# A decoder layer's MLP: the two product chains of a pair of column tiles get PSUM tiles of their own, the first down weights go into the scheduler's order, and a second down tile is begun at each seam

## The chip, the cores and the metric

The kernel runs on one NeuronCore of a Trainium2 chip. The metric is the device time of one execution in microseconds (us), the median of several runs. TensorE (PE) multiplies matrices, VectorE (DVE) and ScalarE (ACT) work element by element, GpSimd (POOL) and SyncE (SP) issue transfers. Each engine works off its own list of instructions, and waits on semaphores for the others.

## The reference, cut to what matters

One layer of a hybrid decoder trunk is applied to 512 prompt tokens and 32 sample tokens. Two mixers and their merge come first, then an MLP with a squared ReLU. The change touches the MLP alone:

```
D_MODEL = 1024
SEQ = 512
DEC_BATCH = 8
DEC_SEQ = 4
D_FF = 4 * D_MODEL
...
    x = x + rms_norm(merged @ w_out, norm_mix_post)
    h2 = rms_norm(x, norm_mlp_pre)
    m = jnp.square(jax.nn.relu(h2 @ w_up)) @ w_down
    x = x + rms_norm(m, norm_mlp_post)
```

Everything is float32.

## The kernel before, in words

Activations lie transposed: 128 channels on the partitions, the 544 tokens along the free axis, in two halves of 272 (`HT`). A float32 product is made of three matmuls on a high and a low part of each operand (`wh`, `wl` of a weight, `bh`, `bl` or `a0h`, `a0l` of an activation): high by high, high by low, low by high. So each weight tile, once it has landed as `wt_...`, is prepared in two steps: ACT copies it into the high part (`cut`, line 1264, "CAST wh"), and DVE subtracts to get the low part (`rest`, line 71, "wl").

`w_up` has 32 column tiles of 128. The first eight are made in the plain way (tiles `ps_u` at lines 116 and 126), scheduled by the framework's list scheduler. From there on the code stands under `tc.manual_schedule`, which keeps each engine's instructions in the order in which the code is written. The rest of `w_up` is done for pairs of column tiles (index `q`, 4 to 15) with seven products instead of eight: `P1` to `P7`, 12 matmuls each (line 1311). They form three accumulation chains. Chain X (P1, P6, P7, P4) and chain Y (P5, P3) lie in one PSUM tile of two banks, `XY[q]`, X in bank 0 and Y in bank 1; chain Z (P2) has a bank of its own. Between the products ACT and DVE read what has accumulated (`keep`, `c11`, `c12`, `c22`, `row1_b`). The order on TensorE for one pair is P6, P1 of the next pair, P7, P2 of the next, P4, P3, P5 of the next. `row1_b` is the ACT instruction at line 1361 that reads X once P4 has ended.

PSUM has two pools: `psd` with two tiles of two banks (`dense_tile`) and `pss` with four tiles of one bank (`scratch`). A dense tile is taken in turn by X/Y of a pair and by the down tiles.

After every four pairs, 1024 rows of the hidden layer are there, and a down pass multiplies them with `w_down`: eight output tiles `m`, each one PSUM tile `ps_d`, eight steps `k` of six matmuls (`d_part`, line 116). `d_load`, `d_cut` and `d_rest` load and prepare the weights of a tile, `d_out` adds the result to what earlier passes gave (ACT copies it in pass 0). There are passes 0 to 3; pass 0 follows the plain part, and pass 3 is of half depth, four steps `k` per tile, and shares a prepared weight between two tiles. The place where the last pair (`p = q + 3`) hands over to the next down pass is called a seam here; there are three. At a seam, steps `k` = 0 to 5 of down tile 0 are interleaved with the last pair's products; steps 6 and 7 need what the last pair yields: `c12` on DVE, `row0`, `act_hi` on ACT, `act_lo` on DVE (the last writes `a0l`).

At the head of the manual part, pass 0 begins. Before its first tile the code writes the loads and the preparation of tile 0, and four DVE instructions on whole quarters (128x1088 elements: `tt_`, `f12`, `f21`), which are operands of the seven products.

Of the kernel before, what the change touches and what calls it, by code (L numbers as in the profile page):

```python
# [13 lines left out]
AF = mybir.ActivationFunctionType  # L14
# [6 lines left out]
NT = 544  # L21
HT = 272
# [23 lines left out]
def layer(ctx, tc, a, o):  # L46
# [1202 lines left out]
    with tc.tile_pool(name="up", bufs=1, reuse_waits="tile") as up:  # L1249
# [50 lines left out]
        def lo(n, q):  # L1300
            W[n, q] = rest(*W[n, q], f"{n}{q}", "b" if n == "B" else "w")

        XY, Z, CP, R = {}, {}, {}, {}

        def product(ps, n, q, half, b, first, last):
            h, l = (w[:, 512 * half:512 * half + 512] for w in W[n, q])
# [4 lines left out]
                    mm(ps, lhsT=w[:, c], rhs=x_[:, k], start=(first and k == 0 and j == 0), stop=(k == 3 and j == 2), skip_group_check=True)  # L1311

        def P1(q):
            XY[q] = dense_tile(f"ps_u{q}")
            product(XY[q][:, 0, 0:HT], "A", q, 0, hb[0, 0], True, False)

        def P2(q):
            Z[q] = scratch(f"ps_uz{q}")[:, 0:HT]
            product(Z[q], "A", q, 1, hb[0, 1], True, True)

        def P3(q):
            product(XY[q][:, 1, 0:HT], "S34", q, 1, hb[1, 1], False, True)

        def P4(q):
            product(XY[q][:, 0, 0:HT], "B", q, 0, tb[4], False, True)

        def P5(q):
            product(XY[q][:, 1, 0:HT], "S12", q, 0, tb[1], True, False)

        def P6(q):  # L1330
            product(XY[q][:, 0, 0:HT], "S12", q, 1, tb[2], False, False)

        def P7(q):
            product(XY[q][:, 0, 0:HT], "S34", q, 0, tb[3], False, False)

        def keep(n, q):
            c = CP[n, q] = up.tile([P, HT], F32, tag=n, name=f"{n}_{q}", bufs=2 if n == "c1" else 1)
            S.copy(c, XY[q][:, 0, 0:HT])

        def res(q):  # L1340
            R[q] = up.tile([P, 2, NT], F32, tag="t", name=f"t_{q}", bufs=2)
# [2 lines left out]
            tt(R[q][:, 0, 0:HT], CP["c1", q], Z[q], ADD)  # L1344

        def c12(q):
            tt(R[q][:, 0, HT:NT], CP["u2", q], XY[q][:, 1, 0:HT], ADD)

        def c22(q):
            tt(R[q][:, 1, HT:NT], CP["u3", q], XY[q][:, 1, 0:HT], ADD)  # L1350

        ak = lambda q, i: ah_[(2 * q + i) % 8]

# [4 lines left out]
            S.activation(R[q][:, 1, HT:NT], R[q][:, 1, HT:NT], AF.Relu, scale=-1.0)  # L1358

        def row1_b(q):  # L1360
            S.activation(R[q][:, 1, 0:HT], XY[q][:, 0, 0:HT], AF.Relu, scale=-1.0)  # L1361
            S.activation(R[q][:, 1], R[q][:, 1], AF.Square)

        def act_hi(q, i):
# [28 lines left out]
        def d_out(c, m):  # L1393
# [3 lines left out]
            else:  # L1397
                tt(mv, ps[:, :, 0:HT], mv, ADD)

        with tc.manual_schedule(engines={ET.PE, ET.Activation, ET.DVE, ET.SP, ET.Pool}):  # L1400
            d_load(0, 0)
            d_load(0, 1)
            d_cut(0, 0)
            d_rest(0, 0)
            d_load(0, 2)

            f11, f21, f12, f22 = (ov[:, 4 * kh:4 * kh + 4, HF[hf]] for hf in range(2) for kh in range(2))
            tt_ = [up.tile([P, 4, HT], F32, tag="t", name=f"tt{i}", bufs=2) for i in range(2)]
            tt(tt_[0], f11, f12, SUB)
            stt(tt_[1], tt_[0], -1.0, f22, MUL, SUB)  # L1410
            tt(f12, f22, f12, SUB)
            stt(f21, tt_[1], -1.0, f21, MUL, SUB)
            d_part(0, 0, *range(8))
            d_cut(0, 1)
            d_rest(0, 1)
            split(*tb[3], f12)
            split(*tb[4], f21)
            d_part(0, 1, *range(8))
            d_load(0, 3)
            d_cut(0, 2)  # L1420
            d_rest(0, 2)
            split(*tb[1], tt_[0])
            d_out(0, 0)
            split(*tb[2], tt_[1])
            d_out(0, 1)
            for c in range(3):

                ms = range(2 if c == 0 else 0, 8)
                q = 4 * c + 4
                nxt = {3: [lambda: load_a(q), lambda: load_s12(q), lambda: load_s34(q), lambda: load_b(q)],  # L1430
                       5: [lambda: add_s(q), lambda: hi("A", q), lambda: lo("A", q), lambda: load_a(q + 1)],
                       6: [lambda: hi("S12", q), lambda: lo("S12", q), lambda: load_s12(q + 1)],
                       7: [lambda: hi("B", q), lambda: lo("B", q), lambda: load_s34(q + 1), lambda: load_b(q + 1)]}
                for m in ms:
                    if m + 2 < 8 and not (c == 0 and m + 2 < 4):
                        d_load(c, m + 2)
                    if m + 1 < 8:
                        if not (c == 0 and m + 1 < 3):
                            d_cut(c, m + 1)
                            d_rest(c, m + 1)  # L1440
                    if c == 0 or m > 1:
                        d_part(c, m, *range(8))
                    elif m == 0:
                        d_part(c, 0, 6, 7)
                    else:
                        d_part(c, 1, *range(8))
                    for f in nxt.get(m, ()):
                        f()
                    d_out(c, m)

                P1(q)
                keep("c1", q)
                P2(q)
                res(q)
                hi("S34", q)
                lo("S34", q)
                hi("A", q + 1)
                c11(q)
                lo("A", q + 1)
                P5(q)  # L1460
                load_a(q + 2)
                for p in range(q, q + 4):
                    n, nn, e = p + 1 < q + 4, p + 2 < q + 4, p == q + 3
                    P6(p)
                    if p > q:
                        hi("B", p)
                        act_hi(p - 1, 0)
                        lo("S34", p)
                    keep("u2", p)
                    if p > q:  # L1470
                        lo("B", p)
                        act_lo(p - 1, 0)
                    if nn:
                        load_s12(p + 2)
                    if n:
                        P1(p + 1)
                        keep("c1", p + 1)
                        add_s(p + 1)
                    if nn:
                        load_s34(p + 2)  # L1480
                        load_b(p + 2)
                    if not n:
                        d_part(c + 1, 0, 0, 1)
                    P7(p)
                    keep("u3", p)
                    c22(p)
                    if n:
                        hi("S12", p + 1)
                        P2(p + 1)
                        res(p + 1)  # L1490
                        c11(p + 1)
                        lo("S12", p + 1)
                    else:
                        d_part(c + 1, 0, 2, 3)
                    row1_a(p)
                    if nn:
                        hi("A", p + 2)
                    P4(p)
                    row1_b(p)
                    if nn:  # L1500
                        lo("A", p + 2)
                    P3(p)
                    act_hi(p, 1)
                    c12(p)
                    row0(p)
                    if p + 3 < q + 4:
                        load_a(p + 3)
                    if n:
                        hi("S34", p + 1)
                        P5(p + 1)  # L1510
                    act_lo(p, 1)
                    if p == q + 1:
                        d_load(c + 1, 0)
                    if p == q + 2:
                        d_load(c + 1, 1)
                        d_cut(c + 1, 0)
                        d_rest(c + 1, 0)
                act_hi(q + 3, 0)
                act_lo(q + 3, 0)
                if c < 2:  # L1520
                    d_part(c + 1, 0, 4, 5)

            wd = []
            xr = {}
            w47 = big.tile([P, 4, 2, 512], F32R, tag="yhg", name="wd47")
            for m in range(8):
                t = mp.tile([P, 2, 512], F32R, tag=f"bl{m // 2}{m % 2}", name=f"wd{m}") if m < 4 else w47[:, m - 4]
                wd.append((t[:, 0], t[:, 1]))
            wt = {}
            for m in range(8):  # L1530
                j = m // 2
                if m % 2 == 0:
                    if j < 2:
                        d_load(3, j + 2)
                    if j < 3:
                        d_cut(3, j + 1)
                        d_rest(3, j + 1)
                    wt[j] = raw(a["w_down2"][1, j].rearrange("p a b c -> p (a b c)"), f"e{j}")
                if m:
                    d_part(3, m, *range(4))  # L1540
                if m % 2:
                    for i in range(2):
                        split(*wd[m - 1 + i], wt[j][:, 512 * i:512 * i + 512])
                d_out(3, m)
                if m > 3:
                    hf, kh = divmod(m - 4, 2)
                    xr[hf, kh] = mp.tile([P, 4, HT], F32, tag=f"bh{hf}{kh}", name=f"xr{hf}{kh}")
                    nc.sync.dma_start(out=xr[hf, kh], in_=x1_d[:, 4 * kh:4 * kh + 4, HF[hf]])
# [152 lines left out]
```

## Time and profile before

| | before |
|---|---|
| median of 3 runs | 988.1 us (988.02 to 989.58) |
| the profiled execution | 985.89 us |
| its span, first to last instruction | 983.9 us |
| PE busy | 952.3 us, 97% |
| DVE busy | 621.6 us, 63% |
| ACT busy | 446.9 us, 45% |
| mean granted TensorE clock | 0.994 |
| share of PE in the chain that ended last | 90% |

The span is what the profile shows instruction by instruction; some 2 us of the execution lie outside it. Matmuls are pipelined, so that PE is shown as busy for longer than the pitch at which matmuls start: a matmul of 272 columns is listed with 290 ns, and the next starts 125 ns after it.

### The profile page before, as it was taken

The page shows a single profiled execution, that of the slowest core. Times are in us where ns is not written, and L with a number is a line of the kernel's source. Part 1 is how long each engine was busy: PE and PEld are TensorE (multiplying, and loading weights), DVE is VectorE, ACT ScalarE, POOL GpSimd, SP SyncE. Part 2 cuts the span into 40 slices and gives each one's busy share as a digit, 9 for nine tenths or more (in the row PEclk, how much of TensorE's full clock was granted, in tenths as well). Part 3 has the DMA queues.
Part 4 walks back from the last instruction along what each step waited for, and adds up shares of the span by engine and source line. Part 5 has one row for each costly group of instructions (what it writes and reads, how often), then busy time and mean ns, then how long its engine had stood idle before and what let it go on. Part 6 is the DMA issues. An engine that isn't in the chain of part 4 may idle for free.

```text
span 983.9 us, 21362 instructions
## 1 busy us (share of the span) xinstructions
PE 952.3 (97%) x9120; PEld 926.6 (94%) x9120; DVE 621.6 (63%) x1158; ACT 446.9 (45%) x834; POOL 62.6 (6%) x104
## 2 busy tenths in 40 slices
PE   8999999999999999999999999899999999999995
PEld 5999999999999999999999999899989998999894
DVE  6877669496774867666477476543753475447647
ACT  6644363644535333663244475333651165126523
POOL 2100000000000001520100000001100110010000
PEclk9999999999999999999999999999999999999998
DMA  7342142242423438554522512444534463355502
GB/s 257 97 132 69 64 156 66 71 131 71 130 66 106 152 130 293 165 183 178 157 70 87 189 43 92 150 103 113 150 115 110 121 153 114 97 138 142 176 2 91
DMA packets 45406, 121.26 MB, mean 123 GB/s; under 512 B 9120, under 2 KB 12576, under 8 KB 44672
## 3 DMA queue, kind: packets, MB, share of 16 engines
q1 hardware_dynamic: 37664, 97.20, 30.8%
q0 software_dynamic: 7360, 22.15, 8.7%
q8 instruction: 71, 1.16, 0.5%
q10 hardware_dynamic: 288, 0.56, 0.2%
q14 instruction: 23, 0.19, 0.1%
HBM read 101.66 MB, written 17.06 MB: 121 GB/s over the span
## 4 chain that ended last, share of the span: by engine, by line
PE 90%; DVE 4%; ACT 3%; issue 1%; DMA 1%; SPq 0%; DVEq 0%; ACTq 0%
PE ps_in L116 27%; PE ps_d L116 17%; PE ps_u L1311 11%; PE ps_u L126 7%; PE ps_bh L116 5%; PE ps_o L116 2%; PE ps_e L126 2%; PE ps_o L126 2%; PE ps_bs L116 2%; PE psL L643 2%; PE ps_uz L1311 2%; PE ps_u L116 1%; PE psO L709 1%; PE psK L693 1%; PE psT L558 1%
## 5 line engine op out<-in xcount | busy, mean ns | idle before, releaser
L116 PE MATMUL ps_in<-hh,wh_in 128*128 128x272 f32 x736 | 159.2, 297 | 0.0
L116 PE MATMUL ps_in<-hl,wh_in 128*128 128x272 f32 x736 | 153.0, 289 | 0.0
L116 PE MATMUL ps_in<-hh,wl_in 128*128 128x272 f32 x736 | 152.3, 288 | 0.0
L116 PEld LDWEIGHTS ps_in<-hh,wh_in 128*128 128x128 f32 x736 | 115.3, 189 | 2.9 <-issue 1.6
L116 PEld LDWEIGHTS ps_in<-hh,wl_in 128*128 128x128 f32 x736 | 115.7, 188 | 0.0
L116 PEld LDWEIGHTS ps_in<-hl,wh_in 128*128 128x128 f32 x736 | 115.6, 189 | 0.0
L71 DVE TENSOR_TENSOR wl_in<-wt_in,wh_in 128x1024 fp32r<-128x1024 f32 (+1 forms) x54 | 61.7, 1144 | 60.6 <-ACT wh_in L99 57.8
L116 PE MATMUL ps_d<-a0h,wh_d 128*128 128x272 f32 x448 | 93.9, 291 | 5.9 <-ACT wh_d L1264 4.2
L116 PE MATMUL ps_d<-a0l,wh_d 128*128 128x272 f32 x448 | 94.2, 292 | 0.5 <-DVE a0l L71 0.5
L116 PE MATMUL ps_d<-a0h,wl_d 128*128 128x272 f32 x448 | 93.7, 291 | 0.5 <-DVE wl_d L71 0.5
L99 ACT CAST wh_in<-wt_in 128x1024 fp32r<-128x1024 f32 x46 | 48.3, 1052 | 97.8 <-PE ps_in L116 93.3
L116 PEld LDWEIGHTS ps_d<-a0h,wh_d 128*128 128x128 f32 x448 | 71.1, 190 | 7.0 <-ACT wh_d L1264 4.7
L116 PEld LDWEIGHTS ps_d<-a0l,wh_d 128*128 128x128 f32 x448 | 71.0, 190 | 0.9 <-DVE a0l L71 0.9
L116 PEld LDWEIGHTS ps_d<-a0h,wl_d 128*128 128x128 f32 x448 | 71.0, 190 | 0.7 <-DVE wl_d L71 0.7
L71 DVE TENSOR_TENSOR ov<-ps_d,ov 128x544 f32<-128x544 f32 x24 | 17.4, 724 | 60.6 <-PE ps_d L116 60.6
L71 DVE TENSOR_TENSOR wl_d<-wt_d,wh_d 128x1024 fp32r<-128x1024 f32 x28 | 34.1, 1219 | 20.8 <-ACT wh_d L1264 20.8
L1264 ACT CAST wh_d<-wt_d 128x1024 fp32r<-128x1024 f32 x28 | 28.7, 1048 | 29.1 <-PE ps_d L116 23.8
L71 DVE TENSOR_TENSOR t<-u,ps_u 128x272 f32<-128x272 f32 x24 | 10.5, 438 | 43.1 <-PE ps_u L1311 27.1
L71 DVE TENSOR_TENSOR wl_S<-wt_S,wh_S 128x1024 fp32r<-128x1024 f32 x24 | 29.3, 1220 | 11.4 <-ACT wh_S L1264 11.4
L1311 PE MATMUL ps_u<-bh,wh_S 128*128 128x272 f32 x96 | 29.0, 302 | 5.8 <-ACT t L1361 5.8
L676 DVE COPY_PREDICATED scT<-masks,psL 32x128 f32<-32x128 uint8 x80 | 28.3, 354 | 2.3 <-PE psS L646 0.2
L1264 ACT CAST wh_S<-wt_S 128x1024 fp32r<-128x1024 f32 x24 | 25.2, 1048 | 10.1 <-PE ps_d L116 10.1
(540 smaller groups left out, 2340.6 us busy)
## 6 DMA issues: line engine op xcount, KB each, us to landing
wt_in<-in_w_in SPq DMA_DIRECT2D x52, 512.0 KB, 3.6
wt_d<-in_w_down SPq DMA_DIRECT2D x28, 512.0 KB, 3.8
wt_A<-in_w_up SPq DMA_DIRECT2D x12, 512.0 KB, 4.0
wt_S<-in_w_up SPq DMA_DIRECT2D x24, 256.0 KB, 2.8
wt_S<-in_w_up POOLq DMA_DIRECT2D x24, 256.0 KB, 4.4
s<-in_hg_s SPq DMA_DIRECT2D x8, 512.0 KB, 3.8
out_hg_s<-s SPq DMA_DIRECT2D x8, 512.0 KB, 4.2
wt_bh<-in_w_br_hg SPq DMA_DIRECT2D x8, 512.0 KB, 3.7
```

Of the source, the lines that this page charges most:

```text
L71: (e or V).tensor_tensor(out=out, in0=x, in1=y, op=op)
L99: S.copy(wh, wt)
L116: mm(ps[:, i, 0:int(np.prod(x[i].shape[1:]))], lhsT=w[:, c], rhs=x[i], start=st, stop=sp)
L126: mm(ps[:, i, 0:HT], lhsT=ws[i][j][:, c], rhs=x[hf], start=st, stop=sp)
L558: nc.tensor.transpose(pt[:, w], src[:, i, w * P:(w + 1) * P], ident)
L643: mm(pq[sq * y:sq * y + m, 4 * i + w], lhsT=k[:, i, c:c + m], rhs=up(c, c + sq, i), start=True, stop=True)
L676: V.copy_predicated(blocks(sc[r], h)[:, :, y, :, 1], masks[r, L].rearrange("p x (n h) -> p x n h", h=h), pq[r].rearrange("p x (n h) -> p x ...
L693: mm(pk[:, w], lhsT=kt2[:, i, w], rhs=vt[:, i, w], start=True, stop=True)
L709: mm(po[:, w], lhsT=sc[:, i, c], rhs=vt[:, i, w], start=True, stop=(w == 0))
L1264: S.copy(h, t)
L1311: mm(ps, lhsT=w[:, c], rhs=x_[:, k], start=(first and k == 0 and j == 0), stop=(k == 3 and j == 2), skip_group_check=True)
```

## The change

X keeps a dense tile, of which it now uses only the first bank; Y moves into a one-bank tile of the other pool, `ps_uy`, taken in P5. The preparation of down tiles 0 and 1 of pass 0 leaves the manual part and goes ahead of it under `high_priority`, so that the list scheduler places it. At each seam the preparation of down tile 1 moves to a place between `row1_a` and P4 of the last pair. In passes 1 and 2, steps 0 to 5 of down tile 1 are put ahead of steps 6 and 7 of down tile 0.

```diff
-            XY[q] = dense_tile(f"ps_u{q}")
-            product(XY[q][:, 0, 0:HT], "A", q, 0, hb[0, 0], True, False)
+            X[q] = dense_tile(f"ps_u{q}")[:, 0, 0:HT]
+            product(X[q], "A", q, 0, hb[0, 0], True, False)
...
-            product(XY[q][:, 1, 0:HT], "S34", q, 1, hb[1, 1], False, True)
+            product(Y[q], "S34", q, 1, hb[1, 1], False, True)
...
-            product(XY[q][:, 1, 0:HT], "S12", q, 0, tb[1], True, False)
+            Y[q] = scratch(f"ps_uy{q}")[:, 0:HT]
+            product(Y[q], "S12", q, 0, tb[1], True, False)
...
+        with tc.high_priority(offset=WAHEAD):
+            for m in range(2):
+                d_load(0, m)
+                d_cut(0, m)
+                d_rest(0, m)
+            d_load(0, 2)
         with tc.manual_schedule(engines={ET.PE, ET.Activation, ET.DVE, ET.SP, ET.Pool}):
-            d_load(0, 0)
-            d_load(0, 1)
-            d_cut(0, 0)
-            d_rest(0, 0)
-            d_load(0, 2)
...
             d_part(0, 0, *range(8))
-            d_cut(0, 1)
-            d_rest(0, 1)
...
                     elif m == 0:
+                        d_part(c, 1, *range(6))
                         d_part(c, 0, 6, 7)
                     else:
-                        d_part(c, 1, *range(8))
+                        d_part(c, 1, 6, 7)
...
                     row1_a(p)
                     if nn:
                         hi("A", p + 2)
+                    if not n:
+                        d_cut(c + 1, 1)
+                        d_rest(c + 1, 1)
                     P4(p)
```

What the scheduler makes of the head of pass 0 stands in no line of the diff. On DVE, at the end of the plain part, the list before has the low part of the first down weight (`wl_d_0`) directly behind the last activation `a0l`:

```order
L71 TENSOR_TENSOR a0l_7266<-t_u_8050,a0h_7265 128x544
L71 TENSOR_TENSOR wl_d_0_8074<-wt_d_0_8068,wh_d_0_8072 128x1024
L71 TENSOR_TENSOR tt_8078<-ov 128x1088
L74 SCALAR_TENSOR_TENSOR tt_8079<-tt_8078,ov 128x1088
L71 TENSOR_TENSOR ov<-ov 128x4x272
L74 SCALAR_TENSOR_TENSOR ov<-tt_8079,ov 128x4x272
L71 TENSOR_TENSOR wl_d_1_8135<-wt_d_1_8070,wh_d_1_8133 128x1024
```

At the same place of DVE's list the changed kernel has:

```order
L71 TENSOR_TENSOR a0l_7266<-t_u_8050,a0h_7265 128x544
L71 TENSOR_TENSOR tt_8082<-ov 128x1088
L74 SCALAR_TENSOR_TENSOR tt_8083<-tt_8082,ov 128x1088
L71 TENSOR_TENSOR ov<-ov 128x4x272
L74 SCALAR_TENSOR_TENSOR ov<-tt_8083,ov 128x4x272
L71 TENSOR_TENSOR wl_d_0_8070<-wt_d_0_8066,wh_d_0_8068 128x1024
L71 TENSOR_TENSOR bl_6966<-ov,bh_6965 128x1088
L71 TENSOR_TENSOR wl_d_1_8076<-wt_d_1_8072,wh_d_1_8074 128x1024
```

`wl_d_0` has moved behind the four instructions on quarters. On ACT the cast `wh_d_0` keeps its place behind the last `a0h`; on PE and SP nothing moves here.

On PE, where P4 of pair 4 ends and its P3 begins (`wh_B` is P4's weight, `bh` and `bl` with `wh_S` are P3's operands), the list before reads, with the semaphores that an instruction waits for behind it:

```order
L1311 MATMUL ps_u_8564<-t_8065,wh_B_8554 128x272 x2
L1311 MATMUL ps_u_8564<-t_8065,wl_B_8556 128x272
L1311 MATMUL ps_u_8564<-bh_6967,wh_S_8593 128x272 [waits Activation_49]
L1311 MATMUL ps_u_8564<-bl_6968,wh_S_8593 128x272
L1311 MATMUL ps_u_8564<-bh_6967,wl_S_8595 128x272
```

And in the changed kernel:

```order
L1311 MATMUL ps_u_8564<-t_8065,wh_B_8554 128x272 x2
L1311 MATMUL ps_u_8564<-t_8065,wl_B_8556 128x272
L1311 MATMUL ps_uy_8602<-bh_6967,wh_S_8593 128x272 [waits DVE_49]
L1311 MATMUL ps_uy_8602<-bl_6968,wh_S_8593 128x272
L1311 MATMUL ps_uy_8602<-bh_6967,wl_S_8595 128x272
```

The products stand in the same order; P3 writes another tile, and waits for DVE (`c22`, the last reader of Y) instead of ACT.

On ACT at the first seam (`u_7` are the `keep` copies of the last pair, `t` the `row1` instructions, `a0h` the high parts of its results), before:

```order
L1338 COPY u_7_9043<-ps_u_8894 128x272
L1358 ACTIVATE t_8941<-t_8941 128x272
L1361 ACTIVATE t_8941<-ps_u_8894 128x272
L1362 ACTIVATE t_8941<-t_8941 128x544
L1365 CAST a0h_7265<-t_8941 128x544
L1365 CAST a0h_7263<-t_8941 128x544
L1264 CAST wh_d_1_9105<-wt_d_1_8990 128x1024
```

And in the changed kernel:

```order
L1339 COPY u_7_9047<-ps_u_8897 128x272
L1359 ACTIVATE t_8944<-t_8944 128x272
L1264 CAST wh_d_1_9063<-wt_d_1_8994 128x1024
L1362 ACTIVATE t_8944<-ps_u_8897 128x272
L1363 ACTIVATE t_8944<-t_8944 128x544
L1366 CAST a0h_7265<-t_8944 128x544
L1366 CAST a0h_7263<-t_8944 128x544
```

The cast of the second down weight has moved ahead of the read of X; its low part moves on DVE in the same way, from behind the last `a0l` to between `c22` and `c12`. On PE, 18 pairs of matmuls of `ps_d_1` (steps 0 to 5) now stand ahead of the six pairs of `ps_d_0` that need the last pair's results. In pass 3, PE's list keeps its order.

## Rows read from the trace of the kernel before

**Rows 1.** Waits of PE, 600 us to the end: total us, times, longest.

```profile
PE ps_u L1311 <- ACT t L1361: 5.8, 12, 0.5
```

**Rows 2.** Timeline of PE, head of pass 0: start us, us, instruction, idle before.

```profile
629.13 0.41 PE L116 MATMUL ps_u<-bh,wl_u 128*128 128x272 f32 x2
632.69 0.52 PE L116 MATMUL ps_d<-a0h,wh_d 128*128 128x272 f32 x2 [3.15 <-ACT wh_d L1264]
...
633.95 0.82 PE L116 MATMUL ps_d<-a0h,wl_d 128*128 128x272 f32 x2 [0.49 <-DVE wl_d L71]
...
635.02 0.65 PE L116 MATMUL ps_d<-a0l,wh_d 128*128 128x272 f32 x2
635.48 0.66 PE L116 MATMUL ps_d<-a0h,wl_d 128*128 128x272 f32 x2
```

**Rows 3.** Windows there: length, PE, PEld, DVE, ACT, POOL busy, clock, DMA share, GB/s.

```profile
634.00:636.00 2.00, 2.00 (x9) 2.00 (x10) 1.97 (x2) 0.00 (x0) 0.00 (x0) 0.50 0.54 106
636.00:638.00 2.00, 2.00 (x14) 2.00 (x14) 2.00 (x3) 0.34 (x1) 0.00 (x0) 0.72 0.42 164
```

**Rows 4.** Timeline of ACT, head of pass 0.

```profile
631.60 1.99 ACT L1264 CAST wh_d<-wt_d 128x1024 fp32r<-128x1024 f32 x2
```

**Rows 5.** Timeline of DVE, head of pass 0.

```profile
632.67 1.23 DVE L71 TENSOR_TENSOR wl_d<-wt_d,wh_d 128x1024 fp32r<-128x1024 f32 x1 [0.22 <-ACT wh_d L1264]
633.82 1.28 DVE L71 TENSOR_TENSOR tt<-ov 128x1088 f32<-128x1088 f32 x1
...
638.75 1.22 DVE L71 TENSOR_TENSOR wl_d<-wt_d,wh_d 128x1024 fp32r<-128x1024 f32 x1
```

**Rows 6.** Timeline of PE, end of P4 and start of P3, pair 4.

```profile
695.54 0.29 PE L1311 MATMUL ps_u<-t,wl_B 128*128 128x272 f32 x1
696.31 0.39 PE L1311 MATMUL ps_u<-bh,wh_S 128*128 128x272 f32 x1 [0.49 <-ACT t L1361]
696.54 0.29 PE L1311 MATMUL ps_u<-bl,wh_S 128*128 128x272 f32 x1
```

**Rows 7.** Timeline of ACT there: `row1_b` reading X.

```profile
695.86 0.40 ACT L1361 ACTIVATE t<-ps_u 128x272 f32<-128x272 f32 x1 [0.43 <-PE ps_u L1311]
```

**Rows 8.** Timeline of DVE there: `c22`, the last reader of Y.

```profile
693.25 0.44 DVE L71 TENSOR_TENSOR t<-u,ps_u 128x272 f32<-128x272 f32 x1 [2.57 <-ACT u L1338]
```

**Rows 9.** Window of one pair, P3 to P3: columns as in rows 3.

```profile
696.31:707.65 11.34, 10.85 (x85) 10.64 (x85) 8.62 (x13) 7.20 (x13) 1.69 (x2) 1.00 0.57 147
```

**Rows 10.** Timeline of PE, first seam: steps 5, 6 and 7 of tile 0, then tile 1.

```profile
733.17 0.41 PE L116 MATMUL ps_d<-a0h,wl_d 128*128 128x272 f32 x2
...
735.22 0.41 PE L116 MATMUL ps_d<-a0h,wl_d 128*128 128x272 f32 x2
...
736.23 0.42 PE L116 MATMUL ps_d<-a0h,wh_d 128*128 128x272 f32 x2
```

**Rows 11.** Timeline of DVE, first seam: `d_out` of tile 0, low part of tile 2's weight.

```profile
736.42 0.72 DVE L71 TENSOR_TENSOR ov<-ps_d,ov 128x544 f32<-128x544 f32 x1 [0.17 <-PE ps_d L116]
737.07 1.22 DVE L71 TENSOR_TENSOR wl_d<-wt_d,wh_d 128x1024 fp32r<-128x1024 f32 x1
```

**Rows 12.** Timeline of PE, third seam: end of P3, down tiles 1 and 2.

```profile
922.18 0.29 PE L1311 MATMUL ps_u<-bh,wl_S 128*128 128x272 f32 x1
923.07 0.52 PE L116 MATMUL ps_d<-a0h,wh_d 128*128 128x272 f32 x2 [0.60 <-DVE t L71]
...
927.44 0.49 PE L116 MATMUL ps_d<-a0h,wh_d 128*128 128x272 f32 x2 [1.09 <-ACT wh_d L1264]
```

**Rows 13.** Timeline of DVE, third seam: the last `a0l` (two), `d_out` of tile 0.

```profile
923.69 1.52 DVE L71 TENSOR_TENSOR a0l<-t,a0h 128x544 fp32r<-128x544 f32 x2
...
926.58 0.72 DVE L71 TENSOR_TENSOR ov<-ps_d,ov 128x544 f32<-128x544 f32 x1
```

**Rows 14.** Timeline of ACT, last pair before the first seam: cast of down weight 0.

```profile
721.15 1.05 ACT L1264 CAST wh_d<-wt_d 128x1024 fp32r<-128x1024 f32 x1
```

**Rows 15.** Timeline of PE there: first use of that weight's low part.

```profile
724.12 0.41 PE L116 MATMUL ps_d<-a0h,wl_d 128*128 128x272 f32 x2
```

More of the change, by code (lines that the diff above doesn't have):

```diff
@@ L1301, in lo @@
             W[n, q] = rest(*W[n, q], f"{n}{q}", "b" if n == "B" else "w")
-        XY, Z, CP, R = {}, {}, {}, {}
+        X, Y, Z, CP, R = {}, {}, {}, {}, {}
         def product(ps, n, q, half, b, first, last):
@@ L1321, in P3 @@
         def P3(q):
-            product(XY[q][:, 1, 0:HT], "S34", q, 1, hb[1, 1], False, True)
+            product(Y[q], "S34", q, 1, hb[1, 1], False, True)
         def P4(q):
-            product(XY[q][:, 0, 0:HT], "B", q, 0, tb[4], False, True)
+            product(X[q], "B", q, 0, tb[4], False, True)
         def P5(q):
-            product(XY[q][:, 1, 0:HT], "S12", q, 0, tb[1], True, False)
+            Y[q] = scratch(f"ps_uy{q}")[:, 0:HT]
+            product(Y[q], "S12", q, 0, tb[1], True, False)
         def P6(q):
-            product(XY[q][:, 0, 0:HT], "S12", q, 1, tb[2], False, False)
+            product(X[q], "S12", q, 1, tb[2], False, False)
         def P7(q):
-            product(XY[q][:, 0, 0:HT], "S34", q, 0, tb[3], False, False)
+            product(X[q], "S34", q, 0, tb[3], False, False)
         def keep(n, q):
             c = CP[n, q] = up.tile([P, HT], F32, tag=n, name=f"{n}_{q}", bufs=2 if n == "c1" else 1)
-            S.copy(c, XY[q][:, 0, 0:HT])
+            S.copy(c, X[q])
         def res(q):
@@ L1346, in c12 @@
         def c12(q):
-            tt(R[q][:, 0, HT:NT], CP["u2", q], XY[q][:, 1, 0:HT], ADD)
+            tt(R[q][:, 0, HT:NT], CP["u2", q], Y[q], ADD)
         def c22(q):
-            tt(R[q][:, 1, HT:NT], CP["u3", q], XY[q][:, 1, 0:HT], ADD)
+            tt(R[q][:, 1, HT:NT], CP["u3", q], Y[q], ADD)
         ak = lambda q, i: ah_[(2 * q + i) % 8]
@@ L1360, in row1_b @@
         def row1_b(q):
-            S.activation(R[q][:, 1, 0:HT], XY[q][:, 0, 0:HT], AF.Relu, scale=-1.0)
+            S.activation(R[q][:, 1, 0:HT], X[q], AF.Relu, scale=-1.0)
             S.activation(R[q][:, 1], R[q][:, 1], AF.Square)
@@ L1437, in layer @@
                     if m + 1 < 8:
-                        if not (c == 0 and m + 1 < 3):
+                        if m and not (c == 0 and m + 1 < 3):
                             d_cut(c, m + 1)
@@ L1534, in layer @@
                         d_load(3, j + 2)
-                    if j < 3:
+                    if 0 < j < 3:
                         d_cut(3, j + 1)
```

## The prediction

> **What bounds the kernel now.** I read the page first: TensorE is busy for 97% of the span and makes 90% of the chain that ended last, so that time can only come from places where TensorE stands still or runs slowly. Next the list of waits, filtered to TensorE and to the MLP (600 us to the end), and then the timeline of each engine around the waits found there. The reader is to see four kinds of gap.
>
> First, one wait that comes twelve times, 5.8 us in sum: P3 waits for an ACT instruction, `t` at line 1361, in each of the twelve pairs [rows 1]. That is `row1_b`, which reads chain X (bank 0) while P3 wants to write chain Y (bank 1 of the same tile).
>
> Second, the head of down pass 0. The last plain matmul starts at about 629.25, the first `ps_d` at 632.69 when `wh_d` is cast, and the first one with the low part `wl_d` at 633.95 [rows 2]. The granted clock behind it is 0.50 (1.2 GHz) and comes back between 636 and 638 [rows 3].
>
> Third and fourth, the seams: at the first two, steps 6 and 7 of down tile 0 wait for the last pair's results [rows 10]; at the third, tile 1 and then tile 2 wait [rows 12].
>
> The steady pitch, for what follows: four pairs of matmuls from 735.22 to 736.23, 0.25 us a pair, 0.125 a matmul [rows 10].
>
> **Part 1, the head of pass 0: a loss.** The order of DVE's list shows `wl_d_0` behind four instructions on quarters, and TensorE's list has the same order as before. Before, DVE was free at 632.45 (it idled 0.22 before 632.67), made `wl_d_0` until 633.90, and TensorE went on 0.05 later [rows 2, 5]. The four instructions took from 633.82 to 638.75, 4.93 us, of which none waited for another engine [rows 5]. Now they start at 632.45 less 0.07 (DVE starts an instruction some 0.08 before the listed end of the one ahead), 632.38; `wl_d_0` runs from 637.31 to 638.54, and TensorE goes on at 638.59 instead of 633.95: **+4.64 us**. Nothing covers it: four matmuls with the high part are all that TensorE has ahead, and its list is in order. `wh_d_0` keeps its place on ACT, so that the first wait, 3.15 us, stays.
>
> Would DVE not take `wl_d_0` first, since its operand is ready at 632.6? The trace has that very case: the second weight's high part was cast by 633.59 (631.60 + 1.99) [rows 4], and its low part ran only at 638.75, behind the four [rows 5]. By the Trainium skill ("PSUM — Partial Sum Buffer", Engine vs sequencer instructions) the queues of VectorE, ScalarE and GpSimd are strictly first in, first out; by that the trace agrees, and were it otherwise this term would be near nothing.
>
> The low clock. It was low from about 634 to 637.1 (a mean of 0.72 in 636 to 638 is 1.1 us at 0.50), some 3.1 us after the restart at 633.95, with a pair of matmuls in 0.46 us instead of 0.25 [rows 2, 3]. Now TensorE restarts later and from a longer pause. If the clock again comes back 3.1 us after the restart, nothing is added; if it comes back as late as it did after the first matmuls (637.1 less 632.69, 4.4 us), 1.3 us more at 1.2 GHz cost 0.6. I take **+0.2**, near the lower end, because the matmuls at 632.69 and the restart were then almost one burst.
>
> **Part 2, X and Y apart: the main gain.** The last matmul of P4 starts at 695.54; P3's second matmul would follow at 695.79 and starts at 696.54 [rows 6]: 0.75 us, more than the 0.49 that is listed as waiting, since the matmul's own end, the semaphore and a slow first matmul (0.23 to the next) are in it. With Y in a tile of its own P3 waits for `c22`, which ended at 693.69, 1.97 us before P3's turn [rows 8], and `row1_b` (695.86 to 696.26) [rows 7] reads beside it. Twelve times 0.75: **-9.0 us**. The chains in `pss` turn round in four tiles, X in `psd` in two as before, so no new wait for a tile comes in the pairs. A pair lasted 11.34 us, in which DVE was busy 8.62, ACT 7.20, and DMA 0.57 of the time [rows 9]; at 10.59 us DVE has 81%, so the shorter pair still holds the work.
>
> By the Trainium skill ("PSUM — Partial Sum Buffer", PSUM bank collisions raise a hardware error) two engines may not touch the same bank and quadrant at once, and accesses to different banks run clean. By that the wait taken away kept apart nothing that the chip needs apart. No run here has shown it yet; a time for such accesses no row gives.
>
> What is late next: the low part of the next pass's first weight. `wh_d` is cast at 721.15 to 722.20, in ACT's run behind P4, which the change does not bring closer [rows 14]; DVE can follow at 722.24 and takes 1.22 [rows 11], TensorE sees it at 723.51. Its turn was 724.12 [rows 15] and is now 0.75 earlier, 723.37: late by 0.14, and a restart costs 0.10 (0.23 instead of 0.125 [rows 6]). Three seams, 0.25 each: **+0.75** (bounds 0 and 1.5, twice that).
>
> **Part 3, seams 1 and 2.** Step 5 ended at 733.42 by pitch, so that the third pair of step 6 was due at 733.92; it started at 735.22 [rows 10]: 1.30 us. Now 18 pairs of tile 1, 4.5 us, stand ahead of it. The results are late by 2.9 us after P3's end at the third seam (925.21, the second of two `a0l` [rows 13], less 922.31, one pitch behind 922.18 [rows 12]); with steps 4 and 5 (1.5 us) the cover is 6.0 us. The tile for it is free when `row1_b` has read X, before P3 ends; its weight is cast between `row1_a` and `row1_b`, where ACT idled 1.69 us, and 1.05 fit. **-2.6 us** for two.
>
> The price: tile 2 has only steps 6 and 7 of tile 1 between itself and the end of tile 0, formerly the whole of tile 1. `d_out` of tile 0 starts 0.19 after the tile's end at 736.23 and ends at 0.91; the low part of weight 2 starts at 0.84 and ends at 2.06, seen at 2.11 [rows 10, 11]. TensorE wants the PSUM tile at 1.5 and that low part at 2.0: late by 0.11, with a restart 0.2. **+0.4** for two (bounds 0 and 1.0).
>
> **Part 4, seam 3.** From P3's end at 922.31, tile 1 started 0.76 later, since it takes the tile of X and Y, which `c12` read last; tile 2 started at 5.13 [rows 12]. That start is put down to ACT, but the cast was ready, and `d_out` of tile 0, which frees the PSUM tile, ended at 927.30, 0.14 ahead [rows 13]. Now tile 1 follows P3 at once, and `d_out` stands directly behind the last `a0l`, whose end is 2.9: it ends at 3.55 and tile 2 starts at 3.69. **-1.45 us**.
>
> **Sum.** +4.64 + 0.2 - 9.0 + 0.75 - 2.6 + 0.4 - 1.45 = **-7.1 us**. The profiled execution, 985.89 us with a span of 983.9, becomes 978.8. It is 2.2 us below the median of the runs, so the median becomes **981.0 us**. With all bounds low the sum is -8.4 (979.7), with all high -5.3 (982.8).
>
> **Rivals.**
> *The pairs give half back.* If in the shorter pair DVE or a transfer comes to its limit, the next product waits instead of P3. For it: DVE at 81% in order, DMA at 0.6 [rows 9]. Against: `c22` is 1.97 us early [rows 8]. Half of 9.0 lost: -2.6, 985.5 us.
>
> *The P3 gain does not come at all* (the two banks still get in each other's way, or another wait stands there): -7.1 + 9.0 = +1.9, 990.0 us. Against it: the row names a semaphore from ACT, and the new list has none.
>
> *Slower by the clock.* Two pauses now follow one another, 3.15 and some 5 us with four matmuls between. By the Trainium skill ("TensorE: Matmul & The Clock Gate", HAM oscillation) pauses between bursts bring TensorE back to the half clock, again and again; by that the trace agrees for one pause, with 0.50 behind it [rows 3]. As a mechanism of this kernel: if the clock stayed at 0.50 beyond 3.1 us after the restart, each further microsecond costs 0.46 [rows 2]. From 7.1 / 0.46, some 15 us, it is a loss; over the whole of pass 0's first half, 30 us, the kernel would take 981.0 + 12.4 = 993.4 us. Against: after 3.15 us of pause it came back in 3.1 us [rows 3].
>
> *The head costs nothing* (DVE has the quarters done in time after all): -11.9, 976.2 us. Against: rows 5.
>
> **Numbers.** Chances: the sum 0.70, half given back 0.14, no P3 gain 0.05, slower by the clock 0.05, head free 0.06. A measurement of this kernel tells about 0.2% (2 us) from no change. Faster than 986.1: the sum, the free head, and nearly all of the half case, 0.88. Within: rest of the half case and most of the third, 0.06. Slower: 0.06. The range 978.5 to 984.8 holds the first case with the scatter of runs (1.6 us here) and a part of the half case; outside are the others.
>
> **What would show it.** Right: no wait of `ps_u` or `ps_uy` on `t` at line 1361, P3 0.125 us behind P4; a wait of some 5 us of `ps_d` on `wl_d` near 633.5, with four DVE instructions of 1.28 ahead of it; no wait on `a0l` at the first two seams; tile 2 of pass 3 starting 3.7 us after P3's end. Wrong: any PE wait above 0.5 us within the pairs, a clock of 0.50 beyond 643, or the first `wl_d` back at 634.

## The result, and the profile after

The changed kernel takes 981.34 us (median of 4 runs, 980.04 to 983.25) against 988.58 us (4 runs, 988.02 to 989.58): a ratio of 0.9927, with a 95% interval of 0.9907 to 0.9948. 981.0 us was predicted, in a range of 978.5 to 984.8.

| | before | after |
|---|---|---|
| the profiled execution | 985.89 us | 980.57 us |
| its span | 983.9 us | 978.5 us |
| PE, DVE, ACT busy | 952.3, 621.6, 446.9 us | 950.3, 621.5, 446.1 us |
| mean granted TensorE clock | 0.994 | 0.991 |
| share of PE in the chain that ended last | 90% | 91% |

The totals tell little: the work is the same. The list of waits of PE in the changed kernel (600 us to the end; total us, times, longest) tells more:

```profile
PE ps_d L116 <- DVE wl_d L71: 4.8, 1, 4.8
PE ps_d L116 <- ACT wh_d L1264: 3.2, 1, 3.2
...
PE ps_d L116 <- DVE ov L71: 0.4, 1, 0.4
```

In the kernel before, the same list has, besides [rows 1]:

```profile
PE ps_d L116 <- ACT wh_d L1264: 4.2, 2, 3.2
PE ps_d L116 <- ACT a0h L1365: 1.0, 2, 0.5
...
PE ps_d L116 <- DVE wl_d L71: 0.5, 1, 0.5
PE ps_d L116 <- DVE a0l L71: 0.5, 2, 0.2
```

The twelve waits of [rows 1] are gone, and so are the waits on `a0h` and `a0l` at the first two seams. The wait on `wl_d` has grown from 0.5 to 4.8 us. The timeline of PE in the changed kernel (start us, us, instruction, idle before) at the places of [rows 2, 6, 10, 12, 15], with the first matmul of each block's first pair and of the end part between them:

```profile
630.38 0.41 PE L116 MATMUL ps_u<-bh,wl_u 128*128 128x272 f32 x2
633.95 0.62 PE L116 MATMUL ps_d<-a0h,wh_d 128*128 128x272 f32 x2 [3.15 <-ACT wh_d L1264]
...
639.83 0.82 PE L116 MATMUL ps_d<-a0h,wl_d 128*128 128x272 f32 x2 [4.80 <-DVE wl_d L71]
...
690.10 0.29 PE L1311 MATMUL ps_u<-bh,wh_A 128*128 128x272 f32 x1
...
702.06 0.29 PE L1311 MATMUL ps_u<-t,wl_B 128*128 128x272 f32 x1
702.19 0.29 PE L1311 MATMUL ps_uy<-bh,wh_S 128*128 128x272 f32 x1
702.31 0.29 PE L1311 MATMUL ps_uy<-bl,wh_S 128*128 128x272 f32 x1
...
728.15 0.41 PE L116 MATMUL ps_d<-a0l,wh_d 128*128 128x272 f32 x2
728.55 0.52 PE L116 MATMUL ps_d<-a0h,wl_d 128*128 128x272 f32 x2
...
745.06 0.41 PE L116 MATMUL ps_d<-a0l,wh_d 128*128 128x272 f32 x2
745.40 0.52 PE L116 MATMUL ps_d<-a0h,wl_d 128*128 128x272 f32 x2
...
781.47 0.29 PE L1311 MATMUL ps_u<-bh,wh_A 128*128 128x272 f32 x1
...
872.84 0.29 PE L1311 MATMUL ps_u<-bh,wh_A 128*128 128x272 f32 x1
...
918.31 0.29 PE L1311 MATMUL ps_uy<-bh,wl_S 128*128 128x272 f32 x1
918.43 0.42 PE L116 MATMUL ps_d<-a0h,wh_d 128*128 128x272 f32 x2
...
922.05 0.49 PE L116 MATMUL ps_d<-a0h,wh_d 128*128 128x272 f32 x2 [0.42 <-DVE ov L71]
...
940.35 0.41 PE L126 MATMUL ps_e<-a0h,wd 128*128 128x272 f32 x2
```

P3 follows P4 at the pitch of 0.125 us (702.06, 702.19, 702.31). In the head the first `wl_d` is used at 639.83 instead of 633.95. At the first seam the low part of the next weight is late by 0.15 (728.55 instead of 728.40, one pitch of 0.25 behind 728.15), and at tile 2 by 0.09 (745.40 instead of 745.31). At the third seam tile 1 follows P3 at once, and tile 2 starts 3.74 behind the start of P3's last matmul, where it was 5.26 in the kernel before [rows 12]. The timelines of DVE and of ACT in the changed kernel show who is behind that:

```profile
633.63 1.28 DVE L71 TENSOR_TENSOR tt<-ov 128x1088 f32<-128x1088 f32 x1
...
637.36 1.28 DVE L74 SCALAR_TENSOR_TENSOR ov<-tt,ov 128x1088 f32<-128x1088 f32 x1
638.56 1.22 DVE L71 TENSOR_TENSOR wl_d<-wt_d,wh_d 128x1024 fp32r<-128x1024 f32 x1
...
919.75 1.52 DVE L71 TENSOR_TENSOR a0l<-t,a0h 128x544 fp32r<-128x544 f32 x2
921.19 0.72 DVE L71 TENSOR_TENSOR ov<-ps_d,ov 128x544 f32<-128x544 f32 x1
```

```profile
702.39 0.40 ACT L1362 ACTIVATE t<-ps_u 128x272 f32<-128x272 f32 x1 [0.43 <-PE ps_u L1311]
```

And the windows of the changed kernel on PE (length, PE busy, granted clock, DMA share, GB/s), as [rows 3]:

```profile
636.00:638.00 2.00, 0.00 (x0) 0.50 0.00 0
...
642.00:644.00 2.00, 2.00 (x11) 0.50 0.71 247
644.00:646.00 2.00, 2.00 (x16) 0.89 0.18 47
```

The clock is back after 644, some 4.6 us behind the restart at 639.83; in the first trace of the kernel before it was 3.1. `wl_d` stands behind the four quarter instructions; `d_out` follows the last `a0l` directly; and `row1_b` reads X from 702.39 to 702.79 while P3 writes Y at full pitch. By the Trainium skill ("PSUM — Partial Sum Buffer", PSUM bank collisions raise a hardware error) accesses of two engines to different banks run clean; by that the trace agrees. The prediction said that no run had shown this yet, but the trace of the kernel before has it too: while `c22` reads Y from 693.25 to 693.69 [rows 8], TensorE writes chain Z, in another bank, at full pitch:

```profile
693.27 0.29 PE L1311 MATMUL ps_uz<-bh,wl_A 128*128 128x272 f32 x1
693.39 0.29 PE L1311 MATMUL ps_uz<-bh,wh_A 128*128 128x272 f32 x1
```

For the comparison of kernels I cut each trace at five starts on PE: the last plain `ps_u`, then the first matmul of the pairs 4, 8 and 12, then the first `ps_e` (the end part). The stretch up to pair 4 is called the head here, and the three behind it blocks; each block holds four pairs, the seam behind them and the down pass that follows. In the kernel before the latter four are:

```profile
683.57 0.29 PE L1311 MATMUL ps_u<-bh,wh_A 128*128 128x272 f32 x1
...
778.77 0.29 PE L1311 MATMUL ps_u<-bh,wh_A 128*128 128x272 f32 x1
...
873.97 0.29 PE L1311 MATMUL ps_u<-bh,wh_A 128*128 128x272 f32 x1
...
945.72 0.41 PE L126 MATMUL ps_e<-a0h,wd 128*128 128x272 f32 x2
```

The stretches in us (the head stretch of before from 629.13 [rows 2]; each row one profiled execution; E1 to E10 are the experiments of the next section):

| | last `ps_u` at | head | block 1 | block 2 | block 3 |
|---|---|---|---|---|---|
| before | 629.13 | 54.44 | 95.20 | 95.20 | 71.75 |
| before, again (E8) | 630.08 | 54.40 | 95.20 | 95.20 | 71.78 |
| after | 630.38 | 59.72 | 91.37 | 91.37 | 67.51 |
| after, again (E9) | 632.14 | 59.42 | 91.36 | 91.37 | 67.50 |
| E1 split only | 630.21 | 54.41 | 92.39 | 92.41 | 70.45 |
| E10 split only, again | 632.72 | 55.30 | 92.39 | 92.40 | 68.98 |
| E2 head only | 633.85 | 59.12 | 95.22 | 95.21 | 71.77 |
| E3 seams only | 632.40 | 55.36 | 94.11 | 94.10 | 70.47 |
| E4 old head | 630.10 | 54.53 | 91.36 | 91.37 | 67.50 |
| E5 early head | 631.01 | 48.88 | 91.37 | 91.37 | 67.50 |
| E6 P3 first | 632.59 | 54.55 | 94.43 | 94.43 | 70.92 |
| E7 no pause | 631.49 | 57.69 | 91.36 | 91.36 | 67.51 |

Two executions of one kernel repeat their blocks to 0.05 us wherever the clock is full, so that each part of the change can be read to a tenth of a microsecond, though runs of one kernel scatter by 1 to 5 us as wholes.

### The profile page after: what moved, and what is told of

The parts are those of the page before. It is cut to its first block, busy times and chain, and to the rows that moved or that the text cites. A ratio compares the mean times of both kernels' runs of the same rounds, so it can differ in the third digit from the quotient of the medians.

```text
span 978.5 us, 21347 instructions
## 1 busy us (share of the span) xinstructions
PE 950.3 (97%) x9120; PEld 927.0 (95%) x9120; DVE 621.5 (64%) x1158; ACT 446.1 (46%) x834; POOL 62.5 (6%) x104
## 4 chain that ended last, share of the span: by engine, by line
PE 91%; DVE 4%; ACT 2%; issue 1%; DMA 1%; SPq 0%; DVEq 0%; ACTq 0%
PE ps_in L116 27%; PE ps_d L116 17%; PE ps_u L1311 7%; PE ps_u L126 7%; PE ps_bh L116 5%; PE ps_uy L1311 4%; PE ps_o L116 2%; PE ps_e L126 2%; PE ps_o L126 2%; PE ps_bs L116 2%; PE psL L643 2%; PE ps_uz L1311 2%; PE ps_u L116 1%; PE psO L709 1%; PE psK L693 1%
## 5 line engine op out<-in xcount | busy, mean ns | idle before, releaser
L116 PE MATMUL ps_bh<-yl,wh_bh 128*128 128x272 f32 x128 | 26.8, 291 | 1.4 <-DVE yl L71 1.4
L116 PE MATMUL ps_bh<-yh,wh_bh 128*128 128x272 f32 x128 | 27.1, 293 | 0.0
```

Of the source, the lines that this page charges most:

```text
L116: mm(ps[:, i, 0:int(np.prod(x[i].shape[1:]))], lhsT=w[:, c], rhs=x[i], start=st, stop=sp)
```

## The experiments

The theory: the change is four independent terms, a loss in the head and three gains (P3's wait, seams 1 and 2, seam 3), which add. The rivals: gains that need each other, a head that is loss of clock or chance, a wait that is not the tile's. Ratios are to the kernel before, with 95% intervals; E8, E9 and E10 are one execution each, without a ratio.

**E1, E2, E3, E4: each part alone, and the change without its head.** E1 is the kernel before with the lines on X and Y alone, E3 with those on the seams alone; their cores are

```diff
-            product(XY[q][:, 1, 0:HT], "S34", q, 1, hb[1, 1], False, True)
+            product(Y[q], "S34", q, 1, hb[1, 1], False, True)
```

```diff
+                        d_part(c, 1, *range(6))
                         d_part(c, 0, 6, 7)
...
+                    if not n:
+                        d_cut(c + 1, 1)
+                        d_rest(c + 1, 1)
                     P4(p)
```

E4 is the changed kernel with the edit below, and E2 the kernel before with its reverse:

```diff
-        with tc.high_priority(offset=WAHEAD):
-            for m in range(2):
-                d_load(0, m)
-                d_cut(0, m)
-                d_rest(0, m)
-            d_load(0, 2)
         with tc.manual_schedule(engines={ET.PE, ET.Activation, ET.DVE, ET.SP, ET.Pool}):
+            d_load(0, 0)
+            d_load(0, 1)
+            d_cut(0, 0)
+            d_rest(0, 0)
+            d_load(0, 2)
...
             d_part(0, 0, *range(8))
+            d_cut(0, 1)
+            d_rest(0, 1)
```

> The kernel before with chains X and Y in PSUM tiles of their own, and nothing else of the change. If the terms of the prediction stand each for itself, twelve waits of 0.75 us go and the low part of the first down weight is late by 0.25 at three seams: -8.25 us from the kernel before, a ratio of 0.9917. In the trace: no wait of ps_u or ps_uy on line 1361, the waits on a0l at the seams as before, the head as before. Rival, the pairs give half back to DVE or a transfer: -4, a ratio of 0.996. Rival, the wait was not what held P3: no change.

> The kernel before with the first two down weights in the scheduler's order, and nothing else of the change. If the head is a loss by itself: +4.64 us of wait for the first low part, and +0.65 us of the 1.2 GHz clock (as the trace of the changed kernel has it: back 4.6 us after the restart, not 3.1), so +5.3 us, a ratio of 1.0054. Rival, the lost time was covered by later work of pass 0, and only the clock costs: +0.7, a ratio of 1.001. Rival, the head in the trace of the changed kernel was late by chance of that execution (its work ahead of the head was 1.26 us later): +4.3, a ratio of 1.0044.

> The kernel before with the new order at the seams alone (second down tile begun ahead of steps 6 and 7 of the first, its weight prepared between the last pair's products), X and Y still in one tile. If the seams' gain stands by itself: 1.30 less 0.2 at each of seams 1 and 2, and 1.45 at seam 3: -3.65 us, a ratio of 0.9963. Rival, the gain at the seams needs the split: with one tile for X and Y the second down tile gets its PSUM tile only after c12, and the cast put ahead of row1_b delays P3 at each seam by up to 1 us: -0.6 to -2, a ratio of 0.998 to 0.9994.

> The changed kernel with the head of pass 0 as it was before (the first two down weights inside the block in written order, the first low part ahead of the four quarter instructions). If the terms add: the changed kernel less 5.3 us, so 11.9 to 12.6 us less than the kernel before, a ratio of 0.9873 to 0.988; the first wl_d wait is gone, and the clock comes back some 3.1 us after the restart. Rival, the later start only moved a stall that comes back elsewhere (a transfer or a weight of pass 0 that is now late): less than 3 us below the changed kernel, a ratio above 0.990.

Measured: E1 979.48 us, 0.9904 (0.9887 to 0.992); E2 992.42 us, 1.0042 (1.0026 to 1.0059); E3 984.73 us, 0.9956 (0.9941 to 0.997); E4 976.83 us, 0.9874 (0.9857 to 0.9892). All four expectations of the theory lie within the intervals, and the rivals of no effect or of a needed partner do not. The table is sharper: the split takes 2.80 us from each of blocks 1 and 2, the seams 1.10, both together 3.83, and the head goes back to 54.53 in E4. In block 3 the parts do not add quite: the seam lines alone take 1.28 us (E3), where 1.45 was expected, because with X and Y in one tile down tile 1 of pass 3 still waits 0.60 us for `c12`, as in [rows 12]. E2's interval can't tell +5.3 from +4.3; its head stretch of 59.12 is 4.68 more than before, so that the wait (4.62) is nearly all of it; heads of one kind scatter by up to 1 us, so that the 0.06 that is left says nothing of the clock.

One number of E1 did not fit: block 3 was 1.30 us shorter instead of 2.75. The first matmul of tile 2 of pass 3 in E1, and its windows on PE:

```profile
920.08 0.49 PE L116 MATMUL ps_d<-a0h,wh_d 128*128 128x272 f32 x2 [1.88 <-ACT wh_d L1264]
```

```profile
920.00:922.00 2.00, 1.92 (x13) 0.85 0.51 178
922.00:924.00 2.00, 2.00 (x11) 0.50 1.05 383
```

With the split alone tile 1 of pass 3 starts at once, while tile 2 starts as late as before, and the two stops of before, with 0.89 us (922.18 to 923.07) and 1.50 us (925.94 to 927.44) between starts, become one of 2.29 (917.79 to 920.08). Behind it the clock fell to 0.50. E10 asks whether it always does.

**E10 and E9: the split alone, and the changed kernel, once more.**

> The split alone (E1), in one more execution. In the first trace TensorE stood still for 2.3 us ahead of the second tile of the last down pass and then ran 3.2 us at 1.2 GHz, which cost 1.5 us of the split's gain. If such a pause brings the low clock each time, the third block is 70.4 us again; if by chance of the execution, it can be 68.9 (71.75 less 2.75 for the waits, and the pause as long as before).

> The changed kernel, unchanged, in one more execution. From the last ps_u to the first pair's product it took 59.72 us in the first trace and 59.12 in E2, with waits of the same length; if the difference is how long the clock stays at 1.2 GHz by chance of the execution, the number here lies between 59 and 60.5 and the three blocks behind it repeat to 0.05 us (91.37, 91.37, 67.51). If the clock's part belongs to the code, it is 59.7 again.

E10's windows on PE at the same place:

```profile
922.00:924.00 2.00, 0.52 (x4) 1.00 0.16 16
924.00:926.00 2.00, 2.00 (x18) 1.00 0.77 299
```

The same stop (2.28 us between starts), no fall of the clock, and block 3 is 68.98, as expected of chance: the low clock cost E1 1.5 us. In E9 the three blocks repeat, and the head is 59.42, between the 59.12 of E2 and the 59.72 of the first trace.

**E7: no pause in the head.** Matmuls whose results nobody reads fill both stops of the changed kernel, 25 ahead of the first `ps_d` and 40 ahead of the first `wl_d`.

```diff
+            fill(25, "fill0")
...
+            fill(40, "fill1")
```

> The changed kernel with 65 matmuls whose result nobody reads in the two pauses of the head (25 ahead of the first ps_d, 40 ahead of the first wl_d). The waits stay as long, but TensorE does not stand still. If part of the head's loss is the low clock: the granted clock stays 1.00 behind the head, and from the last ps_u to the first pair's product it takes 57 to 58 us instead of 59.72, -2 us from the changed kernel, a ratio to the kernel before of 0.990 to 0.991. Rival, the clock costs nothing here: 59.7 us, the time of the changed kernel, 0.9927.

979.03 us, 0.9913 (0.990 to 0.9927); head 57.69. The interval reaches the changed kernel's own ratio, 0.9927, so it is the head's stretch that tells, from one trace. PE's timeline and windows in E7:

```profile
631.74 3.31 PE L1418 MATMUL fill<-bh 128*128 128x272 f32 x25
635.07 0.52 PE L1425 MATMUL ps_d<-a0h,wh_d 128*128 128x272 f32 x2
...
640.95 0.52 PE L1428 MATMUL ps_d<-a0h,wl_d 128*128 128x272 f32 x2
```

```profile
642.00:644.00 2.00, 2.00 (x18) 1.00 0.67 246
```

The way from the first `ps_d` to the first `wl_d` is 5.88 us, as in the changed kernel (633.95 to 639.83); the clock stays at 1.00, where the changed kernel had 0.50 from 636 to 644. So the low clock costs a head of the new kind 1.4 to 2.0 us (59.12 to 59.72 less 57.69). The old kind pays about as much for its own stop: 57.69 less the 4.62 of wait is 53.07, and its heads took 54.40 to 55.36, which is 1.3 to 2.3 more.

**E8: the kernel before, once more.**

> The kernel before, unchanged, to see how two executions of it differ. If the stall of TensorE at 205.7 us in the transposed part (1.2 to 1.7 us in the changed kernel and in E1 to E4, absent in the one trace of the kernel before) is scatter, it can be there: the head then starts 1 us later than in the first trace. If it comes from the changed programs' code, it is absent again. The low clock behind the head lasts 3 to 6 us by execution, not by edit: between the last ps_u and the first pair's product 54.4 to 55.4 us.

986.68 us. In the changed kernel's trace PE's waits between 200 and 215 us are one row, and E8 has the same row word for word, while the first trace of before has none there:

```profile
PE psL L643 <- issue: 1.2, 1, 1.2
```

It lies in a part that no edit touches, and the profile shows nothing that PE waits for. Of the twelve traces of this case only the first one of before is without it; in the others it takes 1.06 to 2.05 us. So the 1.25 us by which the first trace of the changed kernel comes late to the head (630.38 against 629.13) are the execution's, not the change's. The clock makes the scatter larger: behind the stall it stands at 0.50 to 0.60 from 210 to 212 us in E2, E3, E6, E9 and E10 (stalls of 1.50 to 2.05 us), and at 1.00 in the other six (1.06 to 1.33 us). Those five reach the last `ps_u` at 632.14 to 633.85, the other seven traces at 629.13 to 631.49.

**E6: P3 ahead of P4, in one tile.** The kernel before with

```diff
+                    P3(p)
                     P4(p)
                     row1_b(p)
                     if nn:
                         lo("A", p + 2)
-                    P3(p)
```

> The kernel before, X and Y in one tile as before, but P3 issued ahead of P4 in each pair, so that no reader of the tile stands between the two. If the twelve waits were the order of accesses to one tile (P3 behind row1_b) and not the banks or a late weight: no wait on line 1361, -8 us, a ratio of 0.992, like the split alone (E1). Rival, P3 now comes 1.5 us earlier and waits for c22, which was done 1.97 us ahead of its old turn: part of it back, -4 to -7. Rival, only separate tiles help: no change.

986.13 us, 0.9983 (0.9972 to 0.9995): a miss for the theory's 8 us. The gain, 2.2 us, is also less than the rival's 4 to 7, though clear of no change. Waits of PE in E6 from 600 us, and DVE's timeline at the first seam:

```profile
PE ps_d L116 <- ACT wh_d L1264: 6.4, 5, 3.2
PE ps_d L116 <- DVE wl_d L71: 2.0, 4, 0.5
PE ps_d L116 <- ACT a0h L1365: 1.8, 2, 0.9
```

```profile
734.87 0.44 DVE L71 TENSOR_TENSOR t<-u,ps_u 128x272 f32<-128x272 f32 x1 [4.10 <-ACT t L1361]
```

The twelve waits on line 1361 are gone, so they were the order of accesses to one tile. But `row1_b` and the casts behind it on ACT now have no product of their pair behind them on PE: `wh_d_0` is late (0.73 at the first seam, where it was on time), and `c12` starts only when `row1_b` is done. Of the 3.0 us that four waits are worth, a block keeps 0.77 (95.20 to 94.43); the waits on `wh_d`, `wl_d` and `a0h` have grown by 4.5 us in sum (6.4, 2.0 and 1.8 against 4.2, 0.5 and 1.0). Most of the wait is not removed but moved behind the pair. The split takes 2.80 us off a block; there P3 keeps its place, as cover for ACT's work.

**E5: the version that beats both.** The changed kernel, with the eviction of the last plain tile taken into the part of written order, behind the first weight:

```diff
+            d_cut(0, 0)
+            d_rest(0, 0)
...
+            S.activation(u7, ps[:, :, 0:HT], AF.Relu)
+            tt(u7, u7, u7, MUL)
+            split(*ah_[7], u7.rearrange("p a b -> p (a b)"))
             d_part(0, 0, *range(8))
+            d_cut(0, 1)
+            d_rest(0, 1)
             tt(tt_[0], f11, f12, SUB)
...
+            d_cut(0, 2)
             stt(f21, tt_[1], -1.0, f21, MUL, SUB)
...
+            d_rest(0, 2)
+            d_out(0, 0)
```

> The changed kernel with a new head: inside the block in written order ACT casts the first down weight and DVE makes its low part ahead of the eviction of the last plain tile (u7), the second weight's low part comes ahead of the four quarter instructions, the third's between them. If both head waits (3.15 and 4.8 us) are DVE's and ACT's order and nothing else, TensorE goes from the last ps_u into ps_d with no pause and no low clock: from the last ps_u to the first pair's product 49 to 50 us instead of 59.72, so some 10 us less than the changed kernel (971) and 5 less than the version with the old head (E4); ratio to the kernel before 0.982. Rival, the first wait is the transfer of the weight or a memory still in use by the last plain tile: the 3.15 us stay, 976 to 977, a ratio of 0.988. Rival, a later weight of pass 0 comes late in its turn: in between.

970.62 us, 0.9829 (0.9815 to 0.9844). PE's timeline of E5, and DVE's:

```profile
631.01 0.42 PE L116 MATMUL ps_u<-bh,wl_u 128*128 128x272 f32 x2
631.27 0.42 PE L116 MATMUL ps_d<-a0h,wh_d 128*128 128x272 f32 x2
...
631.77 0.42 PE L116 MATMUL ps_d<-a0h,wl_d 128*128 128x272 f32 x2
```

```profile
628.12 1.23 DVE L71 TENSOR_TENSOR wl_d<-wt_d,wh_d 128x1024 fp32r<-128x1024 f32 x1 [0.23 <-ACT wh_d L1263]
```

Both head waits and the low clock are gone, the head stretch is 48.88, 10.8 us less than after and a little below the 49 to 50 that was expected. So both waits were the order of work on ACT and DVE; the rival (a transfer or a memory in use) falls. Both engines had stood idle just ahead of the last plain tile's eviction, as the trace of the changed kernel shows:

```profile
630.89 0.62 ACT L1205 ACTIVATE t_u<-ps_u 128x544 f32<-128x544 f32 x1 [4.39 <-PE ps_u L116]
```

```profile
631.55 0.73 DVE L71 TENSOR_TENSOR t_u<-t_u 128x544 f32<-128x544 f32 x1 [4.29 <-ACT t_u L1205]
```

## Why the prediction was right, step by step

| step | predicted | shown |
|---|---|---|
| head, the wait for `wl_d_0` | +4.64 | +4.62 (5.88 between the first `ps_d` and the first `wl_d`, 1.26 before) |
| head, the low clock | +0.2 | +0.1, with an uncertainty larger than itself: 59.42 less 54.71, the means of the 3 heads of the new kind and the 7 of the old, less 4.62 |
| P3's waits, less `wl_d_0` late at three seams | -8.25 | -8.4 (2.80 a block, third block by E10) |
| seams 1 and 2, less tile 2's wait | -2.2 | -2.1 (92.40 to 91.37, twice) |
| seam 3 | -1.45 | -1.5 (68.98 to 67.51) |
| sum | -7.1 | -7.2 |

The medians differ by 7.2 us. The steps that the text named are there: `wl_d` behind four DVE instructions, no gap at P3, the low part of the next weight late by 0.15 (0.14 was worked out), tile 2 of pass 3 at 3.74 behind P3's last matmul, which is 3.62 behind its end (3.69 was worked out). The prediction read from the second weight in [rows 5] that DVE would not take `wl_d_0` ahead of its turn; E2 shows this by itself. It also let the cast of weight 1 fit ahead of `row1_b` at a seam, since ACT idled there, a row that it did not show:

```profile
729.84 0.40 ACT L1361 ACTIVATE t<-ps_u 128x272 f32<-128x272 f32 x1 [1.69 <-PE ps_u L1311]
```

It fits: in the changed kernel the cast ends at 733.63, and ACT idles 0.75 more until `row1_b` at 734.38.

The clock's term is the weak one: its size agrees, but by luck, and its reason was wrong. I reasoned that the clock comes back 3.1 us after the restart, as in the one trace that I had. In E1 and E10, one kernel with the old head, it comes back some 3.1 and 5.1 us after it (restarts at 635.03 and 637.54; a mean clock of 0.97 from 638 to 640 and of 0.84 from 642 to 644). The first trace of the changed kernel reads +0.65 here (59.72 less 54.44 less 4.62), past my high bound of 0.6, and its clock stood at 0.50 until some 644.4, beyond the 643 that the prediction had named as a sign of being wrong (its head began 1.25 us later, which is most of that, not all). One trace would have passed for the price of the second pause. But heads with the old code read 54.40 to 55.36, those with the new one 59.12 to 59.72: the spread within each kind is as large as the term. What one trace shows of the clock's part is chance of the execution, and the sign was set too close.

The rival of a slower kernel by the clock falls with E7: all of the low clock in the head is worth 2 us, not 12. The rivals of half the pair gain and of none fall with E1, and that of a free head with E2. The margin of the result over the predicted median, 0.3 us, is inside the scatter of the runs (3.2 us). That the forecast came within 0.3 us is therefore luck; that the terms of the waits came within 0.2 us each is not. Where the scatter comes from is shown for a part: the stall of 1.06 to 2.05 us in the untouched part, the low clock behind it in five traces, and the clock behind the head. Why the stall is there in all traces but one, and why its length differs, stays open.

## What to carry to other kernels

The wait between two products that lie in different banks of one tile was a wait of the order of accesses here, and giving each chain a tile of its own took it away; turning the products round mostly moved it, because the product that stood behind was the cover of another engine's work. On an engine that takes its list in order, the first weight of a stage comes as late as everything ahead of it (4.8 us here): look in the list, not at when its operands are ready, and put it into the idle time before (E5 gains 10.8 us that way, more than the change itself). Cut the trace at marks on the bounding engine and compare stretches: these repeated to 0.05 us at full clock where whole runs scattered by 1 to 5, so that terms of 1 us could be told.

## What the runs showed of the hardware

A stop of TensorE of 2.3 us brought the 1.2 GHz clock in one execution (E1, 1.5 us lost) and not in another of the same kernel (E10). By the Trainium skill ("TensorE: Matmul & The Clock Gate", HAM oscillation) waits between bursts bring the half clock back; by that the trace agrees for the head's stops of 3.15 us, behind which the clock was at 0.50 in all ten traces that had them unfilled, and for the 2.3 us stop in one of two. Two executions of one kernel had their first 630 us differ by up to 2.5 us (E1 and E10), and the stall at 205.7 us was absent in one of two traces of the kernel before and present in the ten traces of the other kernels. Much of that difference is this stall and the clock behind it: 1.33 us and 1.00 in E1, 1.85 us and 0.50 in E10.
